# The mask of a head's decays in one VectorE operation, the per-token column in the bias of ScalarE's exponential

## The chip, the core and the metric

The kernel runs on one core of one Trainium2 chip. Its engines work side by side, each through a queue of its own in a fixed order: PE (TensorE, matmuls), DVE (VectorE), ACT (ScalarE), POOL (GpSimd), and SP, which issues the DMAs. The metric is the device time of one execution in microseconds (us).

## The reference: what is computed

One layer over 512 latent tokens and 256 context tokens, D = 1024: modulation and RMSNorm, one input projection that feeds two token mixers (a bidirectional gated DeltaNet with 8 heads and a bidirectional mLSTM with 4), gates, output projection, and a gated MLP with a 3x3 convolution. What matters here is the matrix of decays of a head, in both mixers. In the DeltaNet:

```python
gc = jnp.cumsum(g.astype(f32).reshape(b, h, n, CHUNK), axis=-1)
lower = jnp.tril(jnp.ones((CHUNK, CHUNK), dtype=bool))
decay = jnp.exp(jnp.where(lower, gc[..., :, None] - gc[..., None, :], -jnp.inf))
a_strict = jnp.einsum('bhnld,bhnsd->bhnls', kb, k) * decay
...
attn = jnp.einsum('bhnld,bhnsd->bhnls', q, k) * decay
```

An entry of the decays is the exponential of a term of the row plus a term of the column, and 0 on the masked side. The mLSTM has the same form with its own gates (`exp(d_n - m_t)`).

## The kernel before

Tokens are taken in 6 chunks of 128 (2 of context, 4 of latent tokens). For a head and a direction `d`, `decay_rows` has SP broadcast the row term of all chunks over 128 partitions by one DMA into a tile `E` of 128x768 (name `Eg`; for an mLSTM head the 4 latent chunks, 128x512, name `Em`). `weights` then makes the decays in place: for each chunk one DVE operation adds the per-token column `colA[:, c, d, row]` and takes the minimum with `mask[d]` (0 or -1e30), and one ACT exponential follows over all chunks. A DeltaNet head calls it twice (`decays`, from `gdn_prep`), an mLSTM head twice (from `ml_prep`): 16 calls with 6 chunks and 8 with 4.

Who reads `E`: DVE's products with k k^T (L681) and with q k^T (L690; L973 in the mLSTM), some 20 us later for the DeltaNet heads. L681's result goes to `inverses`: small 48-partition operations on POOL (L749, L751), 60 per head, between two trips through DRAM (`scr`, `scx`). `merges` turns that into the inverse of the chunk on PE, from `y1p` (L794) on, with operands that DVE and ACT copy (`Dm`).

Work around the change. `mixers` walks over heads s. While the scan of head s runs (`gdn_scan`), `drive` mixes in as bulk the preparation of head s+3 (`gdn_prep`): projections `px_k`, `px_q`, `px_v`, `px_z` on PE, the convolution over tokens `conv_silu` (ACT L572, DVE L573 and L574, ACT L575, DVE L576), and the decays. A scan step is a chain over engines: PE `p` (L861), DVE `X` (L865), PE `p` (L869), ACT `v` (L877), PE `p` (L881), DVE `S` (L888). At the start of a head's scan the tail of the head before runs too (`gdn_tail`): ACT sums, DVE `fo` (L910), POOL `fo` (L911), ACT `o` (L914), after which PE can reset the bank `po` (L847).

The order in each queue is laid down when the program is built (`schedule_with_timeline_sim=True`), by a model of when each instruction's operands come; no order is changed at run time. `follow(ins, "v")` adds the edge that an instruction comes behind the scan's last anchor in DVE's queue (`X` or `S`). It doesn't wait for anything else. ACT's instructions in `weights` have no such edge.

Of the kernel before, what the change touches and what calls it, by code (L numbers as in the profile page):

```python
# [12 lines left out]
AF = mybir.ActivationFunctionType  # L13
ALU = mybir.AluOpType
# [3 lines left out]
P = 128  # L18
# [52 lines left out]
class Kern:  # L71
# [547 lines left out]
    def weights(self, E, d, row, g):  # L619

        nc = self.nc
        for c in g:
            self.follow(nc.vector.scalar_tensor_tensor(E[:, c, :], E[:, c, :], self.colA[:, c, d, row : row + 1], self.mask[d], ALU.add, ALU.min), "v")  # L623
        nc.scalar.activation(E[:, g[0] : g[-1] + 1, :], E[:, g[0] : g[-1] + 1, :], AF.Exp)


    def gdn_prep(self, h):
# [853 lines left out]
```

## Time and profile before

| | |
|---|---|
| median of 3 runs | 1422.54 us (1422.49 to 1425.9) |
| the profiled execution | 1424.8 us, span from first to last instruction 1423.0 us |
| granted TensorE clock, mean | 0.962 of full speed |
| busy in the span | PE 1314.4 us (92%), DVE 934.9 (66%), ACT 581.7 (41%), POOL 704.5 (50%) |

Busy time alone doesn't say what sets the end. The chain of work that ended last is followed back from the last instruction, at each step to what released it; PE is most of it, and the other engines come in where PE waits for them.

### The profile page before, as it was taken

What the parts mean: (1) busy time and instruction counts of PE and PEld (TensorE: products, weight loads), DVE (VectorE), ACT (ScalarE), POOL (GpSimd) and SP (SyncE); (2) the same over time, 40 slices, a digit from 0 to 9 for tenths busy, and PEclk for the clock granted to TensorE, in tenths of its full rate; (3) what the DMA queues carried; (4) which work ended last, traced back from release to release, by engine and by line L of the source; (5) the groups of instructions that cost most, each with busy time, mean ns of one, the idle gap of its engine ahead of it and who ended that gap; (6) DMA issues with size and microseconds to landing.
All of it is one profiled execution on the core that took longest, in us unless ns stands there. A gap on an engine that the chain in (4) does not pass through costs nothing.

```text
span 1423.0 us, 21359 instructions
## 1 busy us (share of the span) xinstructions
PE 1314.4 (92%) x7900; PEld 1108.1 (78%) x7900; DVE 934.9 (66%) x1851; ACT 581.7 (41%) x1259; POOL 704.5 (50%) x847
## 2 busy tenths in 40 slices
PE   5988778998999989999899999889989999999997
PEld 4777667887887878888788987668878888888885
DVE  6648884757776773645555367456469879879833
ACT  6455544544554554333333345112234333333331
POOL 4426988456768468423510103770045555455452
PEclk9999889999999999999999999899999999999999
DMA  8424323231332332443423224675524233233221
GB/s 269 125 77 108 78 48 111 79 94 48 86 88 72 94 77 60 122 133 90 127 60 82 60 58 110 160 198 167 194 61 117 89 91 110 82 104 97 96 89 59
DMA packets 232453, 144.81 MB, mean 102 GB/s; under 512 B 32977, under 2 KB 213982, under 8 KB 232350
## 3 DMA queue, kind: packets, MB, share of 16 engines
q1 hardware_dynamic: 232350, 143.46, 35.8%
q8 instruction: 62, 1.02, 0.3%
q14 instruction: 41, 0.34, 0.1%
HBM read 136.04 MB, written 7.39 MB: 101 GB/s over the span
## 4 chain that ended last, share of the span: by engine, by line
PE 56%; POOL 17%; DMA 10%; DVE 8%; ACT 4%; issue 3%; SPq 1%; POOLq 0%; DVEq 0%; ACTq 0%
PE pu L115 11%; POOL gx L751 6%; POOL iv_t L749 6%; PE pd L115 6%; PE pu L116 5%; PE pv L115 3%; PE pd L116 3%; PE px_g L115 3%; DMA oTg<-in_w_ada_dram 2%; PE po L115 2%; PE pv L116 1%; PE py L115 1%; PE px_g L116 1%; DMA cx<-scx 1%; DVE Eg L623 1%
## 5 line engine op out<-in xcount | busy, mean ns | idle before, releaser
L1451 DVE SCALAR_TENSOR_TENSOR y<-pu,fw,y 128x441 f32<-128x441 f32 (+2 forms) x352 | 230.2, 691 | 41.5 <-ACT y L1442 35.7
L751 POOL TENSOR_TENSOR gx<-gx,iv_t 48x30 f32<-48x30 f32 (+14 forms) x240 | 146.2, 609 | 18.2
L749 POOL TENSOR_TENSOR iv_t<-gx 48x30 f32<-48x30 f32 (+14 forms) x240 | 138.4, 577 | 17.9
L1001 POOL TENSOR_TENSOR mkw<-mkt,colB 128x768 f32<-128x768 f32 x8 | 11.9, 1494 | 123.5 <-PE mpc L1022 77.6
L623 DVE SCALAR_TENSOR_TENSOR Eg<-Eg,colA,mask 128x128 f32<-128x128 f32 x96 | 53.4, 625 | 5.4 <-DMA Eg<-gd 5.4
L139 POOL TENSOR_TENSOR rs<-pw_t,mhalf 128x1 f32<-128x1 f32 x14 | 9.2, 654 | 91.9 <-DVE pw_t L138 91.9
L272 POOL TENSOR_TENSOR oTg<-oTg,sc 128x512 f32<-128x512 f32 x22 | 34.2, 1561 | 27.9 <-DMA oTg<-in_w_ada_dram 27.1
L865 DVE SCALAR_TENSOR_TENSOR X<-p,colA,vt 128x128 f32<-128x128 f32 x80 | 24.4, 344 | 26.2 <-PE p L861 26.1
L877 ACT ACTIVATE v<-p,sc 128x128 f32<-128x128 f32 x80 | 25.1, 367 | 36.0 <-PE p L869 34.4
L1442 ACT ACTIVATE y<-pu,fw 128x512 f32<-128x512 f32 x44 | 30.0, 683 | 21.9 <-PE pu L116 15.4
L744 POOL MEMSET gx<- 48x32 f32 x8 | 1.2, 151 | 69.1 <-DMA gx<-scr 69.0
L1393 POOL TENSOR_TENSOR al<-y,ah 128x512 fp32r<-128x512 f32 x22 | 28.6, 1300 | 12.1 <-ACT ah L1392 9.2
L575 ACT ACTIVATE cv_t<-cv_y 128x512 f32<-128x512 f32 (+1 forms) x40 | 21.7, 543 | 31.1 <-DVE cv_y L574 29.5
L881 PE MATMUL p<-v,kt 128*128 128x128 f32 x160 | 28.5, 301 | 5.0 <-ACT v L877 5.0
L881 PEld LDWEIGHTS p<-v,kt 128*128 128x128 f32 x160 | 24.0, 201 | 11.5 <-ACT v L877 9.8
L1026 DVE SCALAR_TENSOR_TENSOR C<-C,ge,mpc 128x257 f32<-128x257 f32 x32 | 15.4, 480 | 26.1 <-PE mpc L1022 26.0
L272 POOL TENSOR_TENSOR gx<-gx,sc 128x512 f32<-128x512 f32 x12 | 13.5, 1131 | 35.2 <-DMA gx<-in_w_ada_dram 35.2
L1403 DVE TENSOR_TENSOR fd_t<-pd,m 128x512 f32<-128x512 f32 x8 | 5.3, 684 | 38.8 <-PE pd L116 38.8
L888 DVE SCALAR_TENSOR_TENSOR S<-S,ge,p 128x128 f32<-128x128 f32 x64 | 19.4, 340 | 17.2 <-PE p L881 16.9
L274 POOL TENSOR_TENSOR oTg<-oTg 128x256 f32<-128x256 f32 (+1 forms) x44 | 30.1, 702 | 0.7
L861 PE MATMUL p<-S,kT 128*128 128x128 f32 x160 | 29.0, 286 | 1.0 <-DVE S L888 0.5
L340 POOL TENSOR_TENSOR hc<-hl_t,hc 128x256 fp32r<-128x256 f32 x8 | 13.1, 1640 | 30.6 <-ACT hc L338 25.9
(1226 smaller groups left out, 4654.9 us busy)
## 6 DMA issues: line engine op xcount, KB each, us to landing
uw<-in_w_ada_dram SPq DMA_DIRECT2D x16, 512.0 KB
oTg<-in_w_ada_dram SPq DMA_DIRECT2D x32, 256.0 KB
Eg<-gd SPq DMA_DIRECT2D x16, 384.0 KB
gx<-in_w_ada_dram SPq DMA_DIRECT2D x23, 256.0 KB
qs<-gd SPq DMA_DIRECT2D x16, 256.0 KB
aw<-in_w_ada_dram SPq DMA_DIRECT2D x9, 256.0 KB
xn<-in_x_dram SPq DMA_DIRECT2D x4, 512.0 KB
Em<-r1d SPq DMA_DIRECT2D x8, 256.0 KB
```

The lines of the kernel that those rows point to most:

```text
L115: for i in (mm(out, lh, rh, start=start, stop=False), mm(out, lh, rl, start=False, stop=False), mm(out, ll, rh, start=False, stop=stop)):
L116: mm(out, ll, rh, start=False, stop=stop)):
L272: eng.tensor_tensor(w, w, self.sc[:, 4 * i : 4 * i + 4, 0:1].broadcast_to([P, 4, P]), ALU.mult)
L274: eng.tensor_tensor(w[:, 0:m, :], w[:, 0:m, :], w[:, m : 2 * m, :], ALU.add)
L623: self.follow(nc.vector.scalar_tensor_tensor(E[:, c, :], E[:, c, :], self.colA[:, c, d, row : row + 1], self.mask[d], ALU.add, ALU.min), "v")
L749: eng.tensor_tensor(t, Bi[:, 0:j, j : j + 1].broadcast_to([48, j, n]), Bi[:, j : j + 1, j + 1 :].broadcast_to([48, j, n]), ALU.mult)
L751: g = eng.tensor_tensor(Bi[:, 0:j, j + 1 :], Bi[:, 0:j, j + 1 :], t, ALU.add)
L861: g = nc.tensor.matmul(p1[:, d, :], kT[:, c * P : c * P + P], S[d], start=True, stop=True)
L881: g = nc.tensor.matmul(p3[:, d, :], kt[:, c, :], v3[d], start=True, stop=True)
L1393: nc.gpsimd.tensor_tensor(al[:, j, :], ys[0], ah[:, j, :].bitcast(F32), ALU.subtract)
L1442: nc.scalar.activation(y, ps, AF.Copy, scale=tap(0, 0))
L1451: g = nc.vector.scalar_tensor_tensor(o, u3[:, r0 + dy : r1 + dy, c0 + dx : c1 + dx], tap(dy, dx), o, ALU.mult, ALU.add)
```

## The change

The DVE operations per chunk (one with a per-partition column and a full mask, `add` then `min`) become one DVE addition per call, over all its chunks, of the mask, broadcast over the chunks. The column goes into the bias of the exponential, which is now one ACT operation per chunk. The `min` is gone: a masked entry is its value minus 1e30, which the exponential takes to 0. The `follow` edge stays on the DVE operation.

```diff
     def weights(self, E, d, row, g):
 
         nc = self.nc
+        e = E[:, g[0] : g[-1] + 1, :]
+        self.follow(nc.vector.tensor_tensor(e, e, self.mask[d].unsqueeze(1).broadcast_to([P, len(g), P]), ALU.add), "v")
         for c in g:
-            self.follow(nc.vector.scalar_tensor_tensor(E[:, c, :], E[:, c, :], self.colA[:, c, d, row : row + 1], self.mask[d], ALU.add, ALU.min), "v")
-        nc.scalar.activation(E[:, g[0] : g[-1] + 1, :], E[:, g[0] : g[-1] + 1, :], AF.Exp)
+            nc.scalar.activation(E[:, c, :], E[:, c, :], AF.Exp, bias=self.colA[:, c, d, row : row + 1])
```

## Rows read from the trace of the kernel before

**Rows 1.** The page, part 4: the chain that ended last, by engine.
```profile
PE 56%; POOL 17%; DMA 10%; DVE 8%; ACT 4%; issue 3%; SPq 1%; POOLq 0%; DVEq 0%; ACTq 0%
```

**Rows 2.** Busy us (x instructions) from 260 to 550: PE, PEld, DVE, ACT, POOL.
```profile
260.00:550.00 290.00, 271.06 (x2155) 233.44 (x2154) 205.42 (x495) 156.43 (x467) 183.21 (x309) 0.96 0.31 78
```

**Rows 3.** PE's waits from 260 to 550: waiting for whom: us, times, longest.
```profile
PE y1p L794 <- DVE Dm L774: 6.6, 5, 2.5
PE p L881 <- ACT v L877: 4.5, 4, 1.9
...
PE px_q L115 <- DVE cv_y L574: 1.7, 2, 1.2
```

**Rows 4.** The chain in order of time, 0 to 620: start, us, what.
```profile
103.62 1.67 DVE Eg L623 x6
105.89 5.73 DVE Eg L623 x6
...
379.13 6.48 DVE Eg L623 x12
...
441.11 4.27 DVE Eg L623 x6
```

**Rows 5.** Line L623: ns min/median/max, and who waited for it (us, times).
```profile
L623 DVE SCALAR_TENSOR_TENSOR Eg<-Eg,colA,mask x96: 339/630/2425, 103.6 to 501.5; 128x128 f32<-128x128 f32 x96
L623 DVE SCALAR_TENSOR_TENSOR Em<-Em,colA,mask x32: 335/344/353, 590.8 to 779.2; 128x128 f32<-128x128 f32 x32
...
  ACT Eg L624: 27.4, 11
```

**Rows 6.** Timeline, 378 to 388 (head 5): start, us, engine; [idle before <- releaser].
```profile
379.05 6.56 DVE L623 SCALAR_TENSOR_TENSOR Eg<-Eg,colA,mask 128x128 f32<-128x128 f32 x12
...
380.53 1.14 ACT L914 ACTIVATE o<-po,fo 128x128 f32<-128x128 f32 x4 [2.60 <-POOL fo L911]
...
380.71 0.61 PE L869 MATMUL p<-X,gx 128*128 128x128 f32 x4
...
382.00 0.65 POOL L751 TENSOR_TENSOR gx<-gx,iv_t 48x234 f32<-48x234 f32 x1
...
382.28 0.64 ACT L877 ACTIVATE v<-p,sc 128x128 f32<-128x128 f32 x2
...
386.06 0.73 PE L115 MATMUL px_q<-hx,wq5h 128*128 128x512 f32 x2 [1.23 <-DVE cv_y L574]
...
387.77 1.23 DVE L105 TENSOR_TENSOR wv5l<-wv5r,wv5h 128x1024 fp32r<-128x1024 f32 x1 [0.52 <-ACT wv5h L104]
...
387.82 1.69 POOL L751 TENSOR_TENSOR gx<-gx,iv_t 48x238 f32<-48x238 f32 x1
```

**Rows 7.** Timeline, 440 to 452 (head 6).
```profile
441.02 8.38 DVE L623 SCALAR_TENSOR_TENSOR Eg<-Eg,colA,mask 128x128 f32<-128x128 f32 x12
...
446.15 0.61 ACT L877 ACTIVATE v<-p,sc 128x128 f32<-128x128 f32 x2
```

**Rows 8.** Timeline, 262 to 272 (head 3).
```profile
268.97 0.75 PE L881 MATMUL p<-v,kt 128*128 128x128 f32 x4 [1.31 <-ACT v L877]
```

**Rows 9.** Line L540: ns min/median/max.
```profile
L540 DVE TENSOR_TENSOR oTg<-oTg,s x1: 949/949/949, 191.8 to 191.8; 64x768 f32<-64x768 f32 x1
```

**Rows 10.** Groups of ACT by form: xcount | busy us, mean ns | idle before.
```profile
L651 ACT ACTIVATE junk<-kt 128x128 bf16<-128x128 f32 x48 | 15.0, 312 | 1.2
...
L624 ACT ACTIVATE Eg<-Eg 128x768 f32<-128x768 f32 x16 | 13.6, 851 | 27.4 <-DVE Eg L623 27.4
...
L914 ACT ACTIVATE o<-po,fo 128x128 f32<-128x128 f32 x32 | 9.1, 368 | 21.9 <-POOL fo L911 21.9
...
L908 ACT ACTIVATE junk<-po 128x128 bf16<-128x128 f32 x32 | 8.9, 278 | 1.5 <-PE po L852 0.6
...
L624 ACT ACTIVATE Em<-Em 128x512 f32<-128x512 f32 x8 | 5.1, 632 | 9.9 <-DVE Em L623 9.9
```

**Rows 11.** Timeline, 102 to 117 (head 0).
```profile
112.82 0.17 DVE L652 TENSOR_SCALAR ssk<-ssk 128x6 f32<-128x6 f32 x1 [0.60 <-ACT junk L651]
```

## The prediction, made before the changed kernel was run

> **What bounds the kernel now.** I read the chain that ended last first [rows 1]: TensorE (PE) is 56% of it, GpSimd (POOL) 17%, VectorE (DVE) 8%, ScalarE (ACT) 4%. So the kernel is bound by PE, with stretches in which PE waits for others. The change touches the decays of the eight DeltaNet heads (0.1 to 0.5 ms) and of the four mLSTM heads (0.6 to 0.8 ms). In the stretch of heads 3 to 7 PE is busy 271.1 of 290 us [rows 2], so at most 19 us of waits can be won there. The waits of PE in that stretch [rows 3] show what it waits for: 6.6 us for the merges' operands, which come from the GpSimd inverse; 4.5 us at L881 for ACT's `v` of L877; 1.7 us for a PSUM bank that DVE's L574 releases. The last two stand behind the decays: in DVE's queue L574 follows the STTs (scalar_tensor_tensor) of L623, in ACT's queue `v` follows the exponential of L624. In a chain of head 5 and one of head 6 the STTs themselves are the piece that sets the end [rows 4].
>
> Why are they slow? The same 128x128 STT has a median of 344 ns on the mLSTM heads (335 to 353) and 630 ns (up to 2425) on the DeltaNet heads [rows 5], where GpSimd is running the inverse. On the timeline of head 5 twelve STTs take 6.56 us while GpSimd operations of 0.65 us go on beside them [rows 6]; in head 6 they take 8.38 us [rows 7]. DVE waits for GpSimd between them. ACT idled 27.4 us in front of the exponentials for them [rows 5].
>
> **The change, part by part.** *DVE.* Per head and direction, six STTs become one TENSOR_TENSOR (TT) over 128x768 with the mask broadcast over chunks; four become one over 128x512 on mLSTM heads. The nearest row is L540, a TT of 64x768 with a broadcast operand: 949 ns [rows 9]. I take 0.95 us alone; the upper bound is 2.0 us, with one wait for a GpSimd operation as long as an STT's worst ordinary one. Two TTs then take 2 to 3 us where twelve STTs took 6 to 8. DVE's busy time falls by some 30 us, which alone is worth nothing: DVE has slack.
>
> *ACT.* One exponential per direction (851 ns for 768 columns, 632 ns for 512 [rows 10]) becomes six (four) of 128 columns with a bias from a [128,1] column. The two rows give 219 ns per 256 columns, so some 195 ns of each are fixed. The trace has no exponential of 128 columns with such a column. An ACTIVATE of 128 columns from SBUF without one takes 312 ns; from PSUM 278 ns without and 368 ns with one (Square against Copy), so a column costs some 90 ns and the new one about 0.40 us. Back to back they overlap: four of L914 with a column take 1.14 us [rows 6], an interval of (1.14-0.37)/3 = 0.26 us; SBUF adds 0.03, so 0.29. Bounds: 0.26, and 0.40 with no overlap. Six take 0.40+5x0.29 = 1.85 us where one took 0.85; twelve take 3.6 us (3.2 to 4.8). Over 16 calls of six and 8 of four that is about 16+5 = 21 us more of ACT. ACT's former wait of 27.4 us covers this in sum, but not in order: what matters is where the scan's `v` stands.
>
> *Where `v` stands.* The order of each queue is fixed when the program is built, by when the builder expects operands. Today ACT has o, exp(d=0), v, exp(d=1) in head 5 [rows 6] and in four other heads. `v` needs PE's L869, which ends at 380.71+0.61 = 381.32 [rows 6], 2.27 us after the first STT starts at 379.05. Twelve uncontended STTs would end later than that (six take 1.67 us in the piece of head 0 that met no GpSimd work [rows 4], so twelve 3.3), which is why `v` was put between the two exponentials. Two TTs end 1.9 us after the start, ahead of `v`. So I expect all twelve new exponentials to stand in front of `v`, unless the builder prefers the scan.
>
> Then `v` starts 3.6 us after the end of `o`, or of the first TT. Head 5: `o` ends at 380.53+1.14 = 381.67, so v at 385.3 against 382.28 [rows 6]: +3.0, less PE's 1.2 us bank wait, which goes: about +1.7. Heads 4 and 7 repeat this order: head 4 +3.0; head 7 +3.0 less its share of the bank wait (1.7-1.2 = 0.5 [rows 3]) = +2.5. Head 6 has no `o` in front: the first TT waits for one GpSimd operation and ends near 442.6, v at 446.2 against 446.15 [rows 7]: 0. In head 3, where the STTs also held v, PE resumed at 268.97 [rows 8]; with the second TT ending near 267.2 and 1.85 us of exponentials behind it, at about 269.3: +0.3. Sum +7.5 us.
>
> *GpSimd.* A long DVE operation with two SBUF inputs holds GpSimd up: beside L105's TT of 1.23 us a GpSimd operation took 1.69 us, 1.04 more than its neighbours' 0.65 [rows 6]. An STT hardly does. At that ratio a 0.95 us TT costs GpSimd 0.8 us. Twelve TTs of heads 2 to 7 fall into an inverse; lower bound 0, upper 12x0.8 = 9.6 us. I put five on the path (one ahead of the `fo` for which `o` waits in heads 4, 5 and 7, two in head 2, where GpSimd is the chain): +4.0.
>
> *Head 0.* The second six STTs took 5.73 us on the chain [rows 4], held by GpSimd, and L652 behind ACT's queue came at 112.82 [rows 11]. A TT that waits for one GpSimd operation of 1.3 us ends by about 108.1 (105.89+1.3+0.95); the twelve exponentials eat part of it; L652 comes near 110.8: -2.0 us, on the way to the first inverse.
>
> *What takes some back.* When PE is late by 3 us in a stage, part of its later 6.6 us of waiting for merges goes, since GpSimd and DMA don't shift by as much. I take half: -3.3.
>
> *mLSTM heads.* Per call ACT takes 1.27 us for 0.63 (+0.64), DVE about 0.7 for four STTs at the pace of 1.67/6, 1.1 (-0.4); eight calls, behind PE's projections: 0. Without that cover it would be about 8x0.24 = +2 us. No DMA, buffer or queue of SP or POOL is moved.
>
> Sum: 7.5+4.0-2.0-3.3 = +6.2 us. The profiled execution took 1424.8 us (span 1423.0, 1.8 us around it), 2.3 above the median of 1422.54; against the median the change gives 1428.7 us.
>
> **A rule that bears on it.** The Trainium skill, "SBUF — State Buffer", section "SBUF: two separate sides", says that DVE operations with two SBUF inputs and GpSimd operations take one shared port pair as an exclusive lock, held for the whole instruction while the other fully blocks. The trace agrees so far: 1.69 us beside a TT, STTs stretched from 344 to 630 ns. By that rule all twelve TTs would block the inverse; the rival "lock" below prices it from rows alone.
>
> **Rivals.**
> 1. *v stays between* the two exponentials. v then starts 1.85 us after `o`: head 3 -1.3 (PE's idle time there [rows 8]), head 4 +1.25, head 5 0, head 6 -1.7 (444.45 for 446.15), head 7 +0.8: -0.95. With GpSimd +4.0 less absorption 2 and head 0 -2.0: about -1, 1421.6 us. For it: today's order. Against: the TTs end before L869.
> 2. *ACT hides its part, DVE's gain counts* (the other side: faster). The exponentials run while ACT waits for `fo` (2.60 us in front of `o` in head 5 [rows 6]), or after v. Then the chain's three long pieces shrink: 5.73 to 2, 6.48 to 2.5, 4.27 to 1.6 [rows 4]: -10.4, 1412 us. It decides if the builder puts the first six ahead of `o`, or v ahead of all.
> 3. *Lock*: the likeliest order, and all twelve TTs delay a GpSimd chain that is on the path: 6.2+9.6-4.0 = +11.8, and less absorbed: 1434 to 1438 us.
> 4. *The change does not do what it says*: the TT meets GpSimd each time and takes 2.0 us; two take 4, still under 6. That moves v by 1 us at most and is inside the ranges.
>
> **How the numbers follow.** Chances: forecast 0.45, v between 0.22, ACT hides 0.23, lock 0.10. A change under 0.3% (4.3 us) cannot be told from none. The forecast's own range is 1424 to 1434 (12 exponentials in 3.2 to 4.8 us, absorption from none to all): 0.34 of it slower, 0.11 same. Rival 1: 0.16 same, 0.06 faster. Rival 2: 0.22 faster, 0.01 same. Lock: 0.08 slower, 0.02 same. Together faster 0.28, same 0.30, slower 0.42. Since both signs hold much, the range reaches from rival 2 to the lock: 1411 to 1437.
>
> **What would show it.** In the changed profile: 16 TTs of 128x768 with a minimum near 0.95 us; 96 exponentials of 128 columns near 0.40 us, 0.29 apart; ACT's wait for DVE at L624 far below 27.4 us; in heads 4, 5 and 7 twelve exponentials ahead of `v`, and PE's wait at L881 for `v` above 4.5 us in the stretch. I am wrong if v stands in front of or between them, if L881's wait shrinks, or if the stretch of heads 3 to 7 gets shorter; also if the new durations lead the builder to reorder work far from this line.

## Result: slower, as forecast, by more than forecast

| | median of the changed kernel, us | median of the kernel before on the same chip, us | ratio, 95% interval |
|---|---|---|---|
| first set | 1436.55 (4 executions) | 1424.22 (4) | 1.0081, 1.0061 to 1.0100 |
| second set | 1432.90 (11 executions) | 1424.77 (29) | 1.0057, 1.0039 to 1.0075 |

The change costs 8 to 12 us where the forecast had 6.2 (1428.7 us). The profiled execution of the first set has a span of 1438.0 us and is the slowest of its four (1439.71 us), that of the second has 1429.0 us. Behind line 623 the changed kernel's lines stand one higher: the exponential is L625, `fo` L912, `o` L915, `v` L878, and the product with `v` L882.

The new operations by line in the changed kernel: ns min/median/max, first and last start, form; and who waited (us, times). They answer to [rows 5, 10].
```profile
L623 DVE TENSOR_TENSOR Eg<-Eg,mask x16: 942/958/2040, 101.9 to 502.6; 128x768 f32<-128x768 f32 x16
L625 ACT ACTIVATE Eg<-Eg,colA x96: 384/398/423, 102.9 to 507.8; 128x128 f32<-128x128 f32 x96
...
  ACT Eg L625: 7.1, 5
```
The sizes are those of the forecast: an addition 0.94 us alone, an exponential 0.40 us, and ScalarE's wait for VectorE down from 27.4 to 7.1 us.

Head 5 of the changed kernel on the timeline, which answers to [rows 6]: start, us, engine; in brackets idle time before and its releaser.
```profile
379.02 3.19 DVE L623 TENSOR_TENSOR Eg<-Eg,mask 128x768 f32<-128x768 f32 x2
380.08 1.31 POOL L750 TENSOR_TENSOR iv_t<-gx 48x228 f32<-48x228 f32 x1
380.66 0.61 PE L870 MATMUL p<-X,gx 128*128 128x128 f32 x4
381.36 1.72 POOL L912 TENSOR_TENSOR fo<-fo,mhalf 128x4 f32<-128x4 f32 x1
383.12 1.14 ACT L915 ACTIVATE o<-po,fo 128x128 f32<-128x128 f32 x4 [5.48 <-POOL fo L912]
384.13 3.61 ACT L625 ACTIVATE Eg<-Eg,colA 128x128 f32<-128x128 f32 x12
384.31 0.38 PE L848 MATMUL po<-zero 128*128 128x512 bf16 x1 [1.65 <-ACT o L915]
387.63 0.36 ACT L878 ACTIVATE v<-p,sc 128x128 f32<-128x128 f32 x1
388.05 1.35 PE L882 MATMUL p<-v,kt 128*128 128x128 f32 x4 [3.36 <-ACT v L878]
```
The same two GpSimd operations in head 5 of the kernel before:
```profile
378.88 0.60 POOL L749 TENSOR_TENSOR iv_t<-gx 48x228 f32<-48x228 f32 x1
379.44 1.05 POOL L911 TENSOR_TENSOR fo<-fo,mhalf 128x4 f32<-128x4 f32 x1
```
The product that `v` reads (L870) ends at 381.27, and `v` starts at 387.63, 6.4 us later; before, it started at 382.28 [rows 6]. Two things fill the gap, one behind the other on ScalarE. `o` starts only at 383.12, 2.6 us later than before (380.53). Of this 1.38 us come from `fo` and the GpSimd operation in front of it: they last 1.31+1.72 = 3.03 us beside the two additions, where they took 0.60+1.05 = 1.65 us. The other 1.2 us were there before the additions: GpSimd starts these two at 380.08 where it started them at 378.88. Then twelve exponentials in a row take 3.61 us. All twelve stand in front of `v` in heads 3 to 7; in head 7 nine of them come ahead of `o` and three behind it.

To compare like with like, the rest of this text cuts each execution at three matmuls: the first with head 3's `wk`, the first with `mwk0` and the first with `mwk3`. Between the first two lie heads 3 to 7. That stretch in the kernel before and in the changed one: start to end, its us, then busy us (x instructions) of PE, PEld (TensorE's weight loads), DVE, ACT, POOL, the granted clock, DMA share and GB/s. Here and in [rows 2] the clock 1.00 is 2.4 GHz and 0.50 is 1.2 GHz.
```profile
258.20:554.40 296.20, 276.94 (x2204) 238.18 (x2204) 207.37 (x499) 159.66 (x476) 187.32 (x314) 0.97 0.31 78
```
```profile
252.60:564.20 311.60, 281.17 (x2207) 241.59 (x2206) 185.61 (x448) 169.21 (x530) 196.75 (x324) 0.94 0.29 74
```
The same work takes 15.4 us longer: 11.1 us more in which PE is idle (30.4 against 19.3) and 4.2 us more in which it is busy, at a lower clock. GpSimd is busy 9.4 us longer, VectorE 21.8 us less. Ten more operations of GpSimd fall between the two cuts, so not all of the 9.4 us is a hold: against the median of the same shape in the kernel before, the operations that run beside the ten additions lengthen by 6.1 us in sum (5.9 in the second execution), where those beside the sixty operations of the kernel before lengthen by 0.3. PE's waits in this stretch of the changed kernel (whom, us, times, longest) answer to [rows 3]; the wait for `o` of the kernel before, not shown there, follows.
```profile
PE p L882 <- ACT v L878: 12.8, 6, 3.4
PE po L848 <- ACT o L915: 9.0, 5, 3.5
PE y1p L795 <- DVE Dm L775: 6.5, 5, 2.0
```
```profile
PE po L847 <- ACT o L914: 3.2, 3, 2.3
```
The wait for `v` grew by 8.3 us over [rows 3] and that for `o` by 5.8; that for Dm stayed; that for the bank of L574 (1.7 us in [rows 3]) is gone.

The clock is the part that no wait shows. Head 5 of the changed kernel in windows of 4 us, columns as above:
```profile
380.00:384.00 4.00, 2.65 (x14) 2.02 (x13) 2.61 (x3) 0.88 (x4) 3.92 (x5) 1.00 0.00 0
384.00:388.00 4.00, 0.38 (x1) 0.00 (x0) 0.00 (x0) 4.00 (x15) 3.55 (x6) 0.80 0.00 0
388.00:392.00 4.00, 3.95 (x11) 3.32 (x12) 1.18 (x3) 0.98 (x3) 3.59 (x6) 0.50 0.01 4
392.00:396.00 4.00, 4.00 (x19) 3.33 (x19) 2.62 (x5) 1.20 (x2) 3.61 (x6) 0.84 0.20 38
```
PE was busy 0.38 us of one window, and its clock then stood at the lower level through the next. On the timeline a pair of px_k products takes 1.20 us there, and 0.61 us ahead of the gap:
```profile
379.98 0.61 PE L115 MATMUL px_k<-hx,wk5h 128*128 128x512 f32 x2
...
389.05 1.20 PE L115 MATMUL px_k<-hx,wk5h 128*128 128x512 f32 x2
```
In the kernel before the four windows of the same times are all at 1.00. Summed over heads 3 to 7 in windows of 2 us, as (1 - clock) x 2 x length, the time at the lower level is 20.5 us before and 37.6 us after.

### The profile page after: what moved, and what is told of

It is laid out like the page before. It is cut to its first block, busy times and chain, and to the rows that moved or that the text cites. A ratio compares the mean times of both kernels' runs of the same rounds, so it can differ in the third digit from the quotient of the medians.

```text
span 1438.0 us, 21360 instructions
## 1 busy us (share of the span) xinstructions
PE 1313.2 (91%) x7900; PEld 1108.6 (77%) x7900; DVE 892.4 (62%) x1747; ACT 601.2 (42%) x1363; POOL 713.4 (50%) x847
## 4 chain that ended last, share of the span: by engine, by line
PE 58%; POOL 16%; DMA 10%; DVE 6%; ACT 6%; issue 3%; SPq 0%; POOLq 0%; DVEq 0%; ACTq 0%
PE pu L115 11%; POOL gx L752 6%; PE pd L115 5%; POOL iv_t L750 5%; PE pu L116 5%; PE pd L116 3%; PE pv L115 3%; PE px_g L115 2%; DMA oTg<-in_w_ada_dram 2%; PE po L115 2%; PE py L115 2%; PE pv L116 1%; PE px_z L115 1%; PE px_v L115 1%; PE px_mo L115 1%
## 5 line engine op out<-in xcount | busy, mean ns | idle before, releaser
L750 POOL TENSOR_TENSOR iv_t<-gx 48x30 f32<-48x30 f32 (+14 forms) x240 | 141.9, 591 | 18.1
L882 PEld LDWEIGHTS p<-v,kt 128*128 128x128 f32 x160 | 24.6, 206 | 28.0 <-ACT v L878 26.4
L882 PE MATMUL p<-v,kt 128*128 128x128 f32 x160 | 29.2, 308 | 15.2 <-ACT v L878 15.1
L866 DVE SCALAR_TENSOR_TENSOR X<-p,colA,vt 128x128 f32<-128x128 f32 x80 | 24.5, 345 | 25.7 <-PE p L862 25.3
L878 ACT ACTIVATE v<-p,sc 128x128 f32<-128x128 f32 x80 | 25.6, 367 | 35.1 <-PE p L870 33.9
L625 ACT ACTIVATE Eg<-Eg,colA 128x128 f32<-128x128 f32 x96 | 29.6, 398 | 7.2 <-DVE Eg L623 7.1
L1027 DVE SCALAR_TENSOR_TENSOR C<-C,ge,mpc 128x257 f32<-128x257 f32 x32 | 15.4, 480 | 27.3 <-PE mpc L1023 27.2
L576 DVE SCALAR_TENSOR_TENSOR kT<-cv_t,cv_y 128x256 f32<-128x256 f32 (+1 forms) x16 | 11.0, 690 | 31.8 <-ACT cv_t L575 31.8
L768 POOL TENSOR_TENSOR qs<-qs,qT 128x512 f32<-128x512 f32 x16 | 21.3, 1334 | 18.0 <-DMA qs<-gd 15.7
```

The costliest lines, as they stand in the source:

```text
L625: nc.scalar.activation(E[:, c, :], E[:, c, :], AF.Exp, bias=self.colA[:, c, d, row : row + 1])
L750: eng.tensor_tensor(t, Bi[:, 0:j, j : j + 1].broadcast_to([48, j, n]), Bi[:, j : j + 1, j + 1 :].broadcast_to([48, j, n]), ALU.mult)
L882: g = nc.tensor.matmul(p3[:, d, :], kt[:, c, :], v3[d], start=True, stop=True)
```

## Experiments

All stretches and waits, for reading what follows. "To head 3", "mLSTM" and "rest" are the parts ahead of and behind heads 3 to 7; "low clock" is the sum just described. All in us, one profiled execution each; the medians are of 4 to 12 executions, for the kernel before of the 23 beside the first experiments and of 10. The sets ran on several chips, on which the median of the kernel before lies between 1422.0 and 1425.8 us; a ratio in the text is against the kernel before on the same chip. A profiled execution need not lie at the median: that of the adds of two chunks, again, took 1427.76 us where the other eleven took at most 1421.64.

| kernel | median | to head 3 | heads 3 to 7 | mLSTM | rest | wait for v | for o | for Dm | low clock |
|---|---|---|---|---|---|---|---|---|---|
| before | 1423.5 | 258.2 | 296.2 | 194.8 | 673.8 | 4.5 | 3.2 | 6.6 | 20.5 |
| before, again | 1425.5 | 255.8 | 296.2 | 194.6 | 677.8 | 4.8 | 3.0 | 7.8 | 20.5 |
| changed | 1436.6 | 252.6 | 311.6 | 195.5 | 678.3 | 12.8 | 9.0 | 6.5 | 37.6 |
| changed, again | 1432.9 | 251.2 | 308.5 | 192.3 | 677.0 | 12.8 | 9.9 | 4.2 | 30.7 |
| exponentials behind v | 1421.0 | 251.3 | 306.7 | 191.5 | 669.1 | none listed | 4.2 | 15.8 | 40.9 |
| two adds, one exponential | 1436.5 | 258.2 | 310.1 | 193.0 | 675.8 | 0.4 | 7.7 | 17.4 | 41.0 |
| exponentials alone | 1422.0 | 252.4 | 298.9 | 192.2 | 676.1 | 9.8 | 10.0 | 1.3 | 21.8 |
| one add, one exponential | 1420.1 | 245.3 | 302.8 | 193.1 | 674.7 | 5.5 | 11.0 | 4.1 | 27.3 |
| short adds, exponentials behind v | 1431.8 | 258.2 | 306.4 | 192.6 | 677.9 | 0.3 | 4.0 | 15.4 | 37.5 |
| adds of two chunks | 1419.9 | 250.6 | 301.6 | 193.0 | 669.4 | 11.3 | 10.4 | 0.4 | 28.7 |
| adds of two chunks, again | 1418.4 | 257.8 | 302.1 | 195.8 | 670.3 | 11.6 | 11.1 | 0.6 | 28.1 |
| half behind v | 1421.3 | 247.9 | 299.8 | 195.3 | 675.2 | 3.0 | 6.0 | 9.5 | 27.3 |
| two chunks, half behind v | 1415.9 | 253.6 | 297.3 | 194.7 | 669.3 | 2.4 | 5.2 | 10.6 | 27.3 |
| nine in front of v | 1421.3 | 249.8 | 305.8 | 194.7 | 669.5 | 10.4 | 14.5 | 0.2 | 29.6 |

How far one execution differs from another of the same kernel is seen in the three pairs: up to 3.1 us in heads 3 to 7, up to 7.2 us ahead of head 3, up to 4.0 us in the rest.

Two theories stood at the start. Q: `v` waits in ScalarE's queue behind twelve exponentials. L: the long additions hold GpSimd, and `fo`, `o` and the inverse come late.

**Exponentials behind v.** In heads 3 to 7 they are issued after the first pair that writes `v`.
```diff
-            self.weights(E[d], d, h, range(NCH))
+            self.weights(E[d], d, h, range(NCH), h < 3)
...
+        for d in range(2) if h >= 3 else ():
+            self.exps(E[d], d, h, range(NCH))
...
+            i = self.nc.scalar.activation(E[:, c, :], E[:, c, :], AF.Exp, bias=self.colA[:, c, d, row : row + 1])
+            self.queue_after(i, self.vact)
```


> The changed kernel, but in heads 3 to 7 the twelve exponentials over Eg are issued on ScalarE behind the first pair of activations that write v, instead of in front of it. The additions on VectorE are those of the changed kernel. Theory Q (ScalarE's queue: v stands behind twelve exponentials of 3.6 us, and TensorE waits for v): TensorE's wait for v at the p <- v,kt products in the delta heads falls from 12.8 us to under 6, heads 3 to 7 give back 8 to 12 us, and the time is 1424 to 1429 us. Theory L (the long additions hold GpSimd, fo and with it o come late, whatever stands behind them on ScalarE): the time stays at 1433 to 1438 us, and the wait of po for o stays near 9 us. A third one (the exponentials merely move, and what reads Eg comes late instead): the wait for v goes, another of the same size at Dm's readers takes its place, 1432 to 1438 us.

Measured: 1420.97 us, ratio 0.9992 (0.9980 to 1.0005). PE's waits in heads 3 to 7 of this kernel:
```profile
PE y1p L804 <- DVE Dm L784: 15.8, 10, 3.1
PE po L857 <- ACT o L924: 4.2, 2, 3.6
```
The wait for `v` went (the list for this stretch has no line for it), as Q had it, and one of 15.8 us for Dm came, as the third theory had it. Heads 3 to 7 still take 306.7 us, 10.5 more than before, and gave back 2 to 5 us where Q had 8 to 12. The total fell by more than this stretch gave back: the rest is 8 to 9 us shorter than in the changed kernel, which none of the theories had (below). So the total alone would have misled.

**Two adds, one exponential.** VectorE's part alone: the column is added in a second long operation, and one exponential over all chunks is left.
```diff
-        for c in g:
-            nc.scalar.activation(E[:, c, :], E[:, c, :], AF.Exp, bias=self.colA[:, c, d, row : row + 1])
+        col = self.colA[:, g[0] : g[-1] + 1, d, row : row + 1].broadcast_to([P, len(g), P])
+        self.follow(nc.vector.tensor_tensor(e, e, col, ALU.add), "v")
+        nc.scalar.activation(e, e, AF.Exp)
```


> VectorE's part alone, with the result kept: the mask is added over all chunks in one operation, the per-token column in a second one, and a single exponential over all chunks follows as in the kernel before. Two long additions instead of one for each call, so twice as many as in the changed kernel. On ScalarE the two exponentials of a head come after the pair that writes v, as the orders of the queues show. Theory Q: v is no longer held by exponentials, VectorE is some 10 us below the kernel before, time 1418 to 1426 us. Theory L: twice the long additions hold GpSimd twice as often: no faster than the changed kernel, 1434 to 1445 us.

Measured: 1436.48 us, ratio 1.0106 (1.0087 to 1.0124). In heads 3 to 7 PE waits 0.4 us for `v` and as follows for Dm and `o`:
```profile
PE y1p L796 <- DVE Dm L776: 17.4, 8, 5.6
PE po L849 <- ACT o L916: 7.7, 3, 4.9
```
This is against Q: nothing stands in front of `v`, and the loss is there all the same. GpSimd is busy 202.7 us in the stretch against 187.3 us before, and its operations beside the twenty additions lengthen by 11.7 us in sum. But the additions are not the main part of the loss: the kernel with the exponentials behind `v`, which has half as many, takes 306.7 us against 310.1 with nearly the same wait for Dm (15.8 and 17.4), and a later run has this wait without any long addition.

**Exponentials alone.** ScalarE's part alone: the mask is added in short operations, a chunk each.
```diff
-        e = E[:, g[0] : g[-1] + 1, :]
-        self.follow(nc.vector.tensor_tensor(e, e, self.mask[d].unsqueeze(1).broadcast_to([P, len(g), P]), ALU.add), "v")
+        for c in g:
+            self.follow(nc.vector.tensor_tensor(E[:, c, :], E[:, c, :], self.mask[d], ALU.add), "v")
```


> ScalarE's part alone, with the result kept: the mask is added chunk by chunk in short operations of 128 columns on VectorE (no long addition is left), and the exponential runs chunk by chunk with the column as its bias. In heads 3 to 7 nine of the twelve exponentials of Eg stand in front of the pair that writes v and three behind it. Theory Q: three quarters of the delay of v is left (nine exponentials are 2.7 us against 3.6 us), so three quarters of the loss of heads 3 to 7: 1430 to 1437 us. Theory L: no long addition, so no late fo: 1422 to 1427 us, and fo is back at 1.0 us.

Measured: 1421.95 us, ratio 1.0002 (0.9990 to 1.0014); `fo` has a median of 1.03 us and at most 1.14. This is as L had it and against Q in the total. But the wait for `v` is still 9.8 us; what fell is the wait for Dm, to 1.3 us, and the low clock, to 21.8 us. Neither theory holds alone.

**One add, one exponential.** As the changed kernel on VectorE, as the kernel before on ScalarE.
```diff
-            nc.gpsimd.memset(m, 0.0)
+            nc.gpsimd.memset(m, -1.0e8)
...
-        for c in g:
-            nc.scalar.activation(E[:, c, :], E[:, c, :], AF.Exp, bias=self.colA[:, c, d, row : row + 1])
+        nc.scalar.activation(e, e, AF.Exp, scale=1.0e-7)
```


> The long addition of the mask as in the changed kernel, but one exponential over all chunks as in the kernel before; the per-token column is left out, and the mask and the exponent are scaled so that every weight is about exp(-10). VectorE does the least of all kernels, ScalarE no more than before. Both exponentials of Eg (0.85 us each by the rows of the kernel before) stand in front of the pair that writes v. Theory Q (ScalarE's queue in front of v): v is delayed by 1.7 us instead of 3.6 us, so heads 3 to 7 lose about 7 us instead of 15 and the time is 1422 to 1430 us. Theory L (the long additions hold GpSimd, and with it fo, o and the chain that leads to Dm): the same additions, the same loss, 1432 to 1438 us, with fo still at 1.6 to 1.8 us in most heads. Theory QL (it takes both: o late by the additions, and a row of exponentials between o and v): the wait for o stays, the wait for v is about half, 1425 to 1432 us.

Measured: 1420.12 us, ratio 0.9962 (0.9944 to 0.9979). Heads 3 to 7 take 302.8 us, 6 to 9 less than the changed kernel; the wait for `v` is 5.5 us, that for `o` 11.0. It is theory QL's pattern, with a lower total (it had 1425 to 1432 us). With the same long additions, 1.6 us of exponentials in front of `v` in place of 3.6 us brings back about half of the loss. The kernel leaves out the per-token column, so it shows times alone. Its total is 0.4% under the kernel before although heads 3 to 7 are 6.6 us longer; in the profiled execution the gain lies ahead of head 3 (245.3 us).

**Short adds, exponentials behind v.** Both edits together, the diffs of the first and of the third experiment.

> Both links taken out together: the mask is added chunk by chunk in short operations on VectorE (as in the run with ScalarE's part alone), and in heads 3 to 7 the twelve exponentials come behind the first pair that writes v. Theory QL and theory Q: TensorE's wait for v goes (under 2 us in heads 3 to 7) and the stretch of heads 3 to 7 is at most that of the kernel before (296.2 us); time 1412 to 1421 us. Theory L: with the long additions already gone nothing is left to win: 1420 to 1424 us, as with the exponentials in front of v.

Measured: 1431.79 us, ratio 1.0055 (1.0035 to 1.0076), a miss for every theory. Heads 3 to 7 take 306.4 us, as with the long additions behind `v` (306.7), with the same wait for Dm (15.4 us). So it is the place behind `v` that brings this wait, not the length of the additions. The 10.8 us between the two medians lie outside this stretch, in the profiled executions: ahead of head 3 (258.2 against 251.3) and in the rest (677.9 against 669.1).

**Adds of two chunks.**
```diff
+        for c in range(g[0], g[-1] + 1, 2):
+            e = E[:, c : c + 2, :]
+            self.follow(nc.vector.tensor_tensor(e, e, self.mask[d].unsqueeze(1).broadcast_to([P, 2, P]), ALU.add), "v")
```


> The changed kernel with each long addition cut in three, of two chunks (256 columns) each. In heads 3 to 7 ten of the twelve exponentials of Eg stand in front of the pair that writes v. It asks from which length an addition holds GpSimd. If the hold is a matter of the whole length (GpSimd gets in between two additions): fo back near 1.0 us and 1421 to 1427 us. If any addition of this kind holds GpSimd for as long as it runs, and the next follows at once: fo at 1.6 us or more, 1432 to 1438 us.

Measured: 1419.88 us, ratio 0.9964 (0.9948 to 0.9981). The six `fo` of the stretch have a median of 1.13 us and a maximum of 1.19 us, against 1.31 and 1.72 in the changed kernel: between two short additions GpSimd gets in. Beside the thirty additions its operations lengthen by 2.4 us in sum, against 6.1. VectorE pays instead: an addition of two chunks takes 0.41 us at least and 0.78 in the median. The stretch takes 301.6 us with ten exponentials in front of `v`, still 5.4 more than before; that the total is lower all the same lies in the rest (669.4 us, see below).

**The changed kernel again.**

> The changed kernel itself once more, with nothing altered, for the spread of its stretches from one profiled execution to another. All theories: 1433 to 1440 us; heads 3 to 7 (from the first product with head 3's wk to the first with mwk0) within 3 us of 311.6 us, fo at 1.6 to 1.8 us in at least three heads, the wait for v near 12.8 us.

Measured: 1432.90 us, 0.1 under the range. Heads 3 to 7 are 308.5 us, 3.1 less than in the first execution, with the same wait for `v` (12.8 us).

These led to a theory Q2: the exponentials' place on ScalarE pulls both ways. In front they delay `v`; behind, PE reaches the products on Dm ahead of the chain that makes it. Three runs test it.

**Half behind v, two chunks and half behind v, nine in front of v.** The first moves only the second direction's six exponentials; the second adds the shorter additions; the third moves only the last three of twelve.
```diff
+        if h >= 3:
+            self.exps(E[1], 1, h, range(NCH), True)
...
+            if behind:
+                self.queue_after(i, self.vact)
```


> The changed kernel with its long additions, but in heads 3 to 7 the six exponentials of the first Eg stay in front of the pair that writes v and the six of the second come behind it, the order that the kernel before had. Theory Q2 (two ends pull at the place of the exponentials on ScalarE: in front they delay v, behind they delay what reads Eg, and through the chain on GpSimd the products on Dm; the long additions as such cost little): the wait for v falls to 5 to 9 us, that for Dm stays under 9 us, heads 3 to 7 take 298 to 304 us, time 1419 to 1427 us. Theory L (the long additions): 1431 to 1437 us, as with the changed kernel.

> As the run with six exponentials in front of v and six behind, but with each long addition cut in three of two chunks. Theory Q2: the order decides and the length of the additions does not, so the same as with the long additions within 4 us, 1417 to 1425 us. Theory L: the cut additions give 1417 to 1422 us where the long ones stay above 1430 us.

> The changed kernel with its long additions, but in heads 3 to 7 only nine exponentials of Eg are issued in front of the pair that writes v and three behind it, the order in which the run with ScalarE's part alone had them. It differs from that run (1422 us) by the length of the additions alone, and from the changed kernel by the place of three exponentials. Theory Q2: 1420 to 1429 us, the wait for v 8 to 11 us. Theory L: 1431 to 1437 us.

Measured: 1421.25 us, ratio 1.0005 (0.9990 to 1.0019); 1415.89 us, 0.9957 (0.9940 to 0.9974); 1421.31 us, 0.9996 (0.9980 to 1.0012). PE's waits in heads 3 to 7 of the first and of the third:
```profile
PE y1p L805 <- DVE Dm L785: 9.5, 7, 2.4
PE po L858 <- ACT o L925: 6.0, 3, 3.5
PE p L892 <- ACT v L888: 3.0, 2, 1.6
```
```profile
PE po L857 <- ACT o L924: 14.5, 6, 4.4
PE p L891 <- ACT v L887: 10.4, 5, 2.5
```
With the long additions untouched, six exponentials put behind `v` take heads 3 to 7 from 308.5 or 311.6 us to 299.8, against 296.2 before. This is as Q2 had it and against L. Q2 missed in detail: the wait for `v` is 3.0 us where it had 5 to 9, that for Dm 9.5 where it had under 9, and the two-chunk kernel is 5.4 us faster where it had at most 4 (its rest is 5.9 us shorter). The kernel with nine in front owes its total to a short rest too (669.5); its stretch gave back 3 to 6 us. The price of the long additions is read from three pairs with the same number in front: nine in front, 305.8 us with long additions and 298.9 with short ones, of which 4.5 us are the wait for `o` (14.5 against 10.0); six in front, 299.8 and 297.3 with additions of two chunks; none in front, 306.7 and 306.4. So it is not a fixed price: it was paid where exponentials and `v` queue up behind `o`.

**Adds of two chunks, again, and the kernel before, again.**

> The run with additions of two chunks once more, unaltered, since it came out 0.36% under the kernel before and is the best that keeps the result. All theories: 1417 to 1423 us, ratio under 1.

> The kernel before, unaltered, for a second profiled execution beside the first: the six kernels with one long addition took 245.3 to 252.6 us up to the first product with head 3's wk, the kernel before 258.2 us, and two executions of one kernel differed there by 7.2 us. If the shorter additions on VectorE win time ahead of head 3: 255 to 262 us again. If the 258.2 us was this one execution: 248 to 254 us. Heads 3 to 7 within 3 us of 296.2 us either way, ratio 1.

Measured: 1418.43 us, ratio 0.9978 (0.9961 to 0.9996), and 1425.52 us, 0.9994 (0.9982 to 1.0006). The gain of two-chunk additions repeats, at 0.2% to 0.4%, but heads 3 to 7 are 5 to 6 us longer than before in both executions; both have a rest of 669 to 670 us. The 258.2 us ahead of head 3 become 255.8, as the first reading had it; by the means of two executions each (257.0 and 251.9) the changed kernel wins about 5 us there. PE's wait for Dm ahead of head 3 is 11.0 and 11.3 us before, 6.1 and 6.9 in the changed kernel. The 5 us are still less than the 7.2 by which the two executions with two-chunk additions differ there, so they are likely, not shown.

**The rest of the kernel.** Five executions have a rest of 669 to 670 us, the other nine one of 674 to 678. In all five a weight load stands in the SP queue in front of a load that waits for a buffer. The kernel before, then the one with nine in front (start, us, queue, transfer):
```profile
885.48 0.37 SPq L96 DMA_DIRECT2D wb_3r<-in_w_branch_gdn_dram  x1
887.04 0.34 SPq L1210 DMA_DIRECT2D x<-gate  x1
899.10 0.37 SPq L267 DMA_DIRECT2D oTg<-in_w_ada_dram  x1
899.56 0.46 SPq L96 DMA_DIRECT2D wb_3r<-in_w_branch_ml_dram  x1
```
```profile
889.16 0.37 SPq L97 DMA_DIRECT2D wb_3r<-in_w_branch_gdn_dram  x1
891.34 0.34 SPq L1220 DMA_DIRECT2D x<-gate  x1
892.72 0.37 SPq L97 DMA_DIRECT2D wb_3r<-in_w_branch_ml_dram  x1
900.08 2.56 SPq L268 DMA_DIRECT2D oTg<-in_w_ada_dram  x3
```
The transfer of oTg at 899.10 was held 11.6 us until GpSimd freed its buffer, with the weights behind it. PE's waits at `pad` for oTg are 10.2 to 13.6 us in the nine and 5.3 to 6.4 in the five. The builder orders this queue anew for each kernel, far from the edited lines. The link was not tested by a run of its own, so it is not shown, and one case goes against it: the kernel with the exponentials alone has the weight load first and still a rest of 676.1 us. The kernel before and the changed one both lie among the nine, so the loss of the change is not in this.

## Why the prediction was right, and what it mis-sized

**The order.** The step that decided was that all twelve exponentials come in front of `v`. The timeline shows it in all five heads, and the run with six in front, which gives back 10 of the 14 us, shows that this order carries the larger part of the loss; nine and two long exponentials in front give back 4 and 7. The reason given for the order, that two additions end ahead of L869, holds for the builder's model, which lays the order down, but not always on the chip: the two additions last 2.0 to 3.2 us instead of 1.9, and in heads 5 and 7 they end 0.9 us behind that product (in head 5 at 382.21 against 381.27). Rival 1 (`v` stays between) has 1421.6 us, and the run with half behind `v` 1421.25; but its heads 3 to 7 are 3.6 us longer than before, so that the totals agree is chance.

**The delay of v: +7.5 us forecast.** This is 9.2 us for `v` less 1.7 for the bank wait. PE's wait for `v` grew by 8.3 us and the bank wait went, so 6.6 us in all. The sum is near by some luck, since the errors of two heads cancel. Head by head the wait for `v` was and is: head 3 1.31 and 3.36 us (put at +0.3), head 4 0.61 and 3.15 (+3.0), head 5 0 and 3.36 (+3.0), head 6 1.91 and 2.14 (0), head 7 0.61 and 0.75 (+3.0). In head 3 the term missed that `o` itself comes late: it starts 3.0 us after the first addition, where it started 0.4 us after the first STT. In head 7 nine exponentials run ahead of `o`, and the loss stands in the wait for `o` (0.33 and 2.21 us).

**GpSimd: +4.0 forecast.** Beside two additions two operations of head 5 lengthened by 1.38 us, 0.69 an addition against the 0.8 assumed, and beside all ten of the stretch 0.6 an addition; PE's wait for `o` grew by 5.8 us (6.9 in the second execution). The step that put additions ahead of `fo` in heads 4, 5 and 7 was right in kind, and heads 3 and 6 have them too: in heads 3, 5 and 6 `fo` itself is held (1.61 to 1.72 us), in heads 4 and 7 two operations ahead of it (in head 4 1.38 and 1.26 us for 0.62 and 0.66). The Trainium skill, "SBUF — State Buffer", section "SBUF: two separate sides", has the other engine blocked for the whole instruction. As an estimate by that rule, two additions of 0.95 us would cost GpSimd up to 1.9 us; the trace agrees with a hold of most of that time (1.38 us). The rival that priced this rule on all twelve additions (1434 to 1438 us) holds the first median and not the second, and its mechanism does not carry the loss: with the long additions kept and six exponentials put behind `v`, heads 3 to 7 are 3.6 us longer than before, not 14.

**Absorption: -3.3 forecast.** This step failed in part: the wait for Dm is 6.5 us where it was 6.6, in the second executions 4.2 where it was 7.8, so -1.9 by the means. The forecast had GpSimd's chain shift less than PE. A likely reason, not tested, is that the additions that make `o` late hold that chain too.

**The clock: not in the sum.** It is the missing term. Gaps of 3 us and more on PE were priced at their length, but behind them the clock stays low: PE's busy time for nearly the same matmuls (2204 and 2207) rose by 4.2 us, in the second execution by 2.2.

**Head 0: -2.0 forecast, about -0.3 measured.** What L652 was in the kernel before starts at 109.65 against 112.82 [rows 11]. But the DMA that brings Eg had landed earlier in that execution: its first addition starts at 101.90 where the first STT started at 103.62. From there to the first product with Eg it is 9.86 us in the changed kernel, 10.14 before (9.87 and 10.15 in the second executions). By that count the successor of L652 (L653) does start 1.45 us earlier, but it lasts 1.08 us where L652 lasted 0.17, and most of the gain is gone. The first products, in the changed kernel and in the one before:
```profile
111.76 0.34 DVE L682 SCALAR_TENSOR_TENSOR gx<-pkk,sc,Eg 128x128 f32<-128x128 f32 x1
```
```profile
113.76 0.34 DVE L681 SCALAR_TENSOR_TENSOR gx<-pkk,sc,Eg 128x128 f32<-128x128 f32 x1
```
So most of the 5 us ahead of head 3 must come from elsewhere. **mLSTM: 0 forecast**, -0.8 us by the means.

Sum by the means of two executions each: -5.1 ahead of head 3, +13.9 in heads 3 to 7 (10.6 idle, 3.3 busy), -0.8 and +1.8 behind them, +9.8 us; the medians give +12.3 and +8.1. The mechanism in heads 3 to 7 was the one forecast; the mis-sized terms are the wait for `o`, the absorption, the clock and head 0. Heads 2 to 7 were put at 7.5+4.0-3.3 = +8.2 us, and heads 3 to 7 alone cost 13.9; that the total is off by only 2 to 6 us is owed in part to the part ahead of head 3, which no term had at that size.

**Open.** Why Dm is waited for when all exponentials come behind `v` was not settled. It is not that Eg comes late for it: in head 3 of that kernel PE waits 3.85 us for Dm at 22 us after the first product with head 3's `wk`, and the products with head 3's Eg start only at 35.6, so this wait belongs to an earlier head, whose exponentials were not moved. In heads 5 to 7 the products with Eg start at 24.5, 24.2 and 25.4 us, against 27.1, 27.7 and 27.9 in the kernel before. The loss itself lies in heads 3 and 4 (65.4 and 61.6 us against 57.7 and 58.0). It looks as if PE were ahead there and the chain through GpSimd and the transfer of cx were not; this was not tested. Nor was the order of the SP queue tried alone.

## What to carry to other kernels

Cutting one engine's work can cost time by what becomes ready at once: two adds in place of twelve made a row of twelve exponentials that then stood in front of the scan's `v`, and a saving of 22 us on VectorE became a loss of 14 us on TensorE. When an operation is split, ask what the last of its parts stands in front of, and cut the long partner that holds a neighbour: with two chunks an addition and half of the exponentials behind `v` heads 3 to 7 take 297.3 us, nearly what they took before (296.2). That this kernel is 0.43% faster than before in total, the best that keeps the result, is not owed to that stretch but mostly to the rest (669.3 us against 674 to 678). So compare kernels by stretches between the same two instructions: here the total moved by some 7 us in a place that the edit never touched.

## What the hardware showed beyond what was expected

In head 5 TensorE ran 0.38 us of work between 382.66 and 388.05 us; from 388 on it had 4 us at half clock and part of the next 4; a pair of products there took 1.20 us in place of 0.61. So in this kernel a wait costs more than its length. An addition of 768 columns (0.95 us) on VectorE stretched two GpSimd neighbours by 0.7 us each, while additions of 256 columns (0.41 us alone) left `fo` at 1.13 us against its 1.01. Over heads 3 to 7 GpSimd's operations beside the additions lengthened by 6.1 us with ten long ones and by 2.4 with thirty short ones, which VectorE paid for: a short addition of that kernel took 0.78 us in the median. So cutting an operation in three took most of the hold off GpSimd and made VectorE wait instead.
